# A hybrid RWKV-7 and sparse-attention layer: transposes of both heads in one bunch, value products in three bunches a pair, and fill work dealt out anew around the seam

## The chip, the cores and the metric

The kernel runs on one core of a Trainium2 chip. The metric is the device time of one execution in microseconds (us). The engines of the core are named as in the profile: PE (TensorE: matmuls and transposes into PSUM), PEld (its weight loads), DVE (VectorE), ACT (ScalarE), POOL (GpSimd, which here only touches SBUF) and SP (SyncE, which here issues most DMAs). Each engine works through its own instructions in the order in which they were issued.

## The reference

One decoder layer over 512 tokens of 1024 channels, in float32. Both mixers read one projection of the normalised stream:

```python
z = h @ w_in[l]
z_rwkv, z_nsa, z_gate = jnp.split(z, [RWKV_COLS, RWKV_COLS + NSA_COLS], axis=-1)
o_a = rwkv7_time_mix(z_rwkv, ...)
o_b = nsa_attention(z_nsa, ...)
g_a, g_b = jnp.split(jax.nn.sigmoid(z_gate), 2, axis=-1)
m = g_a * (o_a @ w_branch_rwkv[l]) + g_b * (o_b @ w_branch_nsa[l])
x = x + rms_norm(m @ w_out[l], norm_mix_post[l])
...
x = x + rms_norm((jax.nn.silu(u_gate) * u_val) @ ffn_down[l], norm_ffn_post[l])
```

`rwkv7_time_mix` is a linear recurrence over tokens with 16 heads of 64 channels. `nsa_attention` has 16 heads of 64, and its result is the gated sum of three causal attentions: over 31 compressed blocks, over selected blocks and over a sliding window. With 512 tokens the selection takes all blocks and the window reaches back to the start, so the last two are both plain causal attention, with keys and values of their own.

## The kernel before

Everything lies transposed, channels on the 128 partitions and the 512 tokens along the free axis. Large products are split: a float32 operand becomes a high and a low part in the type fp32r, and three matmuls (high by high, high by low, low by high) stand for one. Weights come by DMA as `raw`, ACT makes the high part, POOL the low part (line 160), both into rings of three buffers. A projection of 128 columns is 8 steps of 3 matmuls of 128x512 (lines 290 to 292).

The program is written as Python generators that are advanced in turn; a scheduler then sets the final order on each engine. `drive(fill, *threads)` advances the fill by one step and each thread at its own rate. "Fill" is work that PE can do at almost any time: the 16 sigmoid gates (`gates_`, outputs gt), the projections for q (`qproj`, one for each pair of heads), k and v, and the RWKV half of the branch product (`branch(0, ..)`, outputs ub00 to ub07, 24 matmuls each).

The stages in question:

- RWKV works on two groups of four head pairs (p = 0 to 3 and 4 to 7). Per pair, `prep` and `couple` build the operands: transposes into pb (line 140), then AR on DVE (line 549), then the products g from AR and KB (line 587). One gate is the fill beside the last pair of a group. Then `core(g)` inverts small triangles and runs the recurrence over eight chunks. Beside `core(0)` stand `NG0` = 10 gates and the inputs of pair 4; beside `core(1)` the last 4 gates, four v and two k projections and q0 to q3. `finish` normalises the output of a group and multiplies it by its gate (lines 817 to 849); for group 1 it runs beside the start of the attention.
- The seam: `score0` computes the scores of attention pair 0 with two steps of fill after each block; `vload` transposes the values (vtp).
- The attention runs over eight pairs of heads, p8 = 0 to 7. `score(p8 + 1)` and `values(p8)` are interleaved by a sorted list of fractions of a pair, with some steps of fill (table `FILL2`, with 16 for pairs 0 and 1). `score`: products s of q and k into the two banks of tag px, DVE adds the bias and takes the minimum (line 1056), ACT takes the exponent (line 1058), and `norm` scales each block by gate over sum, half of it on DVE and half on POOL (line 1034). `values`: the compressed part is transposed into pct and evicted as a split pair; then, in five groups `GRP` of one or two (branch, key block) parts, the blocks are transposed into pt (tag py, two banks), evicted into PT (six buffers, on ACT for the groups in `ONACT`, else on DVE), and multiplied by the values into acc, named o (line 1087). These products are float32 with 64 output columns a head; the two heads of a pair stand side by side in the array.
- Before pair `PX` = 2 all remaining fill is run (`run(fill)`), and `load_branch(0, ..)` starts to load RWKV's output and to split it into hh and hl (ACT line 1129, DVE line 1130), which the projections no longer need from there on. From pair 2 on the fill is `branch(0, ..)`.
- After pair 7 the rest of the fill runs, then `load_branch(1, ..)` splits the attention's output into sp, then `branch(1, ..)` (ub10 and on) follows.

In `values` each head's transposes are a step of their own, and the products of the group before stand between head 0's transposes and their eviction:

```python
if e == 0:
    products()
m.append(nw.tile([128, S], F32, tag="PT", name=f"PT{p8}{e}{k}", bufs=6))
```

Of the kernel before, what the change touches and what calls it, by code (L numbers as in the profile page):

```python
# [34 lines left out]
ID, IE, RD, RR, NG0, NQ1, PX, FN = (36, 36), (60, 60), (74, 74), (1.05, 0.85), 10, 4, 2, 1.6  # L35
NW, NU, PA = 13, 3, 0.25
GRP = (((0, 2), (1, 2)), ((0, 1), (0, 3)), ((0, 0),), ((1, 1), (1, 3)), ((1, 0),))
ONACT, FILL2 = (0, 2, 4, 5, 6, 8), (0, 0, 9, 10, 10, 10, 10, 15)
# [4 lines left out]
def hybrid_layer(ctx: ExitStack, tc: tile.TileContext, a, out, dbg=None, stop=None):  # L43
# [831 lines left out]
    for g in range(2):  # L875
        group_tiles(g)
        for i in range(GP):
            p = GP * g + i
            fill = [inputs(p + 1, os_[p + 1])] if i < GP - 1 else gates_(1)
# [60 lines left out]
    drive(itertools.chain(*gates_(16 - 2 - NG0, zp), *fr1, *[qproj(i) for i in range(NQ1)]), f0, *rt1)  # L940
# [72 lines left out]
    def score(p8, o):  # L1013
# [11 lines left out]
        def norm(e, qb):  # L1025
# [5 lines left out]
            for b in range(2):  # L1031
                for k in (qb + 1, qb):
                    i = b * 4 + k
                    (po if b else ve).tensor_scalar(o.pe[e, b, k], o.pe[e, b, k], st[e][:, 3, i:i + 1], None, op0=OP.mult)  # L1034
# [32 lines left out]

    def values(p8, o):
        g = p8 // 2
        acc = pz(f"o{p8}")  # L1070
        pt = py(f"pct{p8}")
# [5 lines left out]
        todo = []  # L1077

        def products(last=False):
            if not todo:  # L1080
                for x in range(2):
                    te.matmul(acc, vcp[:, g, x, :], pct, start=x == 0, stop=False)
                return
            m, parts = todo.pop()
            for b, j, c, n in parts:
                for e in range(2):
                    te.matmul(acc[e * 64:e * 64 + 64, j * 128:], vt[:, j, b * 256 + g * 64:b * 256 + g * 64 + 64],  # L1087
                              m[e][:, c:c + n], start=False, stop=last)

        for k, grp in enumerate(GRP):  # L1090
            m = []
            for e in range(2):
                pt = py(f"pt{p8}{e}{k}")
                parts, c = [], 0
                for b, j in grp:
# [6 lines left out]
                if e == 0:  # L1102
                    products()
# [5 lines left out]
                yield  # L1109
            todo.append((m, parts))  # L1110
        products(True)
        if p8 == 7:
            o.acc = acc
            return
        o8 = nw.tile([128, S], F32, tag="o8", name=f"o8{p8}", bufs=1)
        sc.activation(o8, acc, AF.Copy)
        sc.dma_start(obd[p8], o8)
# [14 lines left out]
    def branch(x, o8, sh, sl):  # L1132
# [3 lines left out]
        wh, wl = wslice(wh), wslice(wl)  # L1136
        p = pj(f"ub{x}{o8}")
# [22 lines left out]
    def score0():  # L1160
        for _ in score(0, os_[0]):
            for _ in range(2):
                next(fill, None)
            yield
# [347 lines left out]
```

## Time and profile before

| what | value |
|---|---|
| median of 3 runs | 1202.02 us (1200.98 to 1203.12) |
| profiled execution | 1201.8 us, its span 1200.0 us |
| RWKV up to the seam | 0 to about 502 us |
| score 0 and attention pairs 0 to 7 | about 502 to 739 us |
| branch products, output projection, MLP | about 739 to 1200 us |
| transposes pt of the attention, line 140 | 320, mean 274 ns |
| value products, line 1087 | 256 in the trace (each is two passes), mean 452 ns |

A row of the timeline or the chain begins with the start and the duration in us. The durations of single matmuls overlap, since PE pipelines them, so what one costs is read from the distance between starts, or from the chain of waits. "Waited for" means that PE stood idle until the engine named was done.

### The profile page before, as it was taken

The page shows a single profiled execution, that of the slowest core. Times are in us where ns is not written, and L with a number is a line of the kernel's source. Part 1 is how long each engine was busy: PE and PEld are TensorE (multiplying, and loading weights), DVE is VectorE, ACT ScalarE, POOL GpSimd, SP SyncE. Part 2 cuts the span into 40 slices and gives each one's busy share as a digit, 9 for nine tenths or more (in the row PEclk, how much of TensorE's full clock was granted, in tenths as well). Part 3 has the DMA queues.
Part 4 walks back from the last instruction along what each step waited for, and adds up shares of the span by engine and source line. Part 5 has one row for each costly group of instructions (what it writes and reads, how often), then busy time and mean ns, then how long its engine had stood idle before and what let it go on. Part 6 is the DMA issues. An engine that isn't in the chain of part 4 may idle for free.

```text
span 1200.0 us, 19851 instructions
## 1 busy us (share of the span) xinstructions
PE 1169.2 (97%) x7414; PEld 928.8 (77%) x7414; DVE 583.1 (49%) x1196; ACT 583.3 (49%) x1141; POOL 587.5 (49%) x529
## 2 busy tenths in 40 slices
PE   8999999999999999989999999999999999999997
PEld 6888878777877887767666776888888888888886
DVE  4225554537465452576777774754334333431103
ACT  5546553346665334466656664543444444443311
POOL 4336654445565444475465752621356655654440
PEclk8999999999899999999999999999999999999999
DMA  6522335411333553345332223751133333334421
GB/s 221 134 76 82 87 95 165 132 51 36 103 117 97 164 144 116 120 139 174 106 106 80 68 66 124 227 197 45 45 97 97 96 98 99 98 93 134 135 66 70
DMA packets 95651, 131.95 MB, mean 110 GB/s; under 512 B 34177, under 2 KB 37057, under 8 KB 95298
## 3 DMA queue, kind: packets, MB, share of 16 engines
q1 hardware_dynamic: 79634, 116.26, 32.0%
q10 hardware_dynamic: 15920, 14.42, 3.8%
q8 instruction: 58, 0.95, 0.3%
q14 instruction: 39, 0.32, 0.1%
HBM read 108.30 MB, written 19.14 MB: 106 GB/s over the span
## 4 chain that ended last, share of the span: by engine, by line
PE 84%; DVE 7%; issue 3%; ACT 3%; POOL 2%; DMA 1%; SPq 0%; DVEq 0%; POOLq 0%; ACTq 0%
PE pu L212 6%; PE pu L214 6%; PE pu L213 6%; PE dn L1245 3%; PE dn L1243 3%; PE dn L1244 3%; PE o L1087 3%; PE pt L140 3%; PE ub L1139 2%; PE ub L1140 2%; PE ub L1141 2%; PE v L290 2%; PE v L291 2%; PE v L292 2%; PE gt L292 2%
## 5 line engine op out<-in xcount | busy, mean ns | idle before, releaser
L1058 ACT ACTIVATE p<-p,stt 128x384 f32<-128x384 f32 (+3 forms) x128 | 70.8, 555 | 54.7 <-DVE stt L1056 54.3
L1034 POOL TENSOR_SCALAR p<-p,stt 128x512 f32<-128x512 f32 (+1 forms) x64 | 74.4, 1171 | 32.8 <-DVE stt L1029 25.2
L1383 DVE SCALAR_TENSOR_TENSOR u<-pu,cvec,u 128x511 f32<-128x511 f32 x44 | 33.0, 749 | 101.5 <-ACT u L1382 101.5
L1056 DVE CUSTOM_DVE_ANT_0 p<-s,rh 128x384 f32<-128x384 f32 (+3 forms) x128 | 58.5, 485 | 28.7 <-PE s L1051 17.4
L1087 PE MATMUL o<-PT,vt 128*64 128x384 f32 (+3 forms) x256 | 50.7, 452 | 1.1 <-DVE PT L1108 1.1
L140 PE MATMUL pt<-ident,p 128*128 128x128 f32 x320 | 49.1, 274 | 0.0
L1387 POOL TENSOR_TENSOR u<-u,u 128x512 f32<-128x512 f32 x22 | 28.4, 1290 | 38.3 <-DVE u L1384 37.3
L140 PEld LDWEIGHTS pt<-ident,p 128*128 128x128 f32 x320 | 39.8, 141 | 8.5 <-issue 0.4
L1389 DVE TENSOR_TENSOR al<-u,ah 128x512 fp32r<-128x512 f32 x22 | 23.9, 1085 | 45.5 <-ACT ah L1388 45.5
L1051 PE MATMUL s<-kst,qs 128*128 128x512 f32 (+1 forms) x128 | 36.9, 387 | 1.2 <-DVE stt L1056 0.8
L1382 ACT ACTIVATE u<-pu,cvec 128x512 f32<-128x512 f32 x44 | 33.6, 764 | 5.1 <-PE pu L1347 5.1
L1106 ACT ACTIVATE PT<-pt 128x512 f32<-128x512 f32 x48 | 28.0, 583 | 14.3 <-PE pt L140 12.2
L1034 DVE TENSOR_SCALAR p<-p,stt 128x512 f32<-128x512 f32 (+1 forms) x64 | 33.9, 563 | 0.9
L1384 DVE SCALAR_TENSOR_TENSOR u<-pu,cvec,u 128x510 f32<-128x510 f32 x44 | 33.0, 749 | 1.6
L1087 PEld LDWEIGHTS o<-PT,vt 128*64 128x64 f32 x256 | 16.9, 136 | 19.9 <-issue 14.5
L1108 DVE COPY PT<-pt 128x512 f32<-128x512 f32 x32 | 22.0, 687 | 18.4 <-PE pt L140 18.3
L1051 PEld LDWEIGHTS s<-kst,qs 128*128 128x128 f32 x128 | 22.7, 190 | 8.2 <-DVE stt L1056 2.8
L587 PEld LDWEIGHTS g<-AR,KB 64*128 64x128 f32 x256 | 19.8, 187 | 10.6 <-DVE GS L590 4.2
L1291 DVE TENSOR_TENSOR p2tm<-dn,gb 128x512 f32<-128x512 f32 x4 | 2.8, 692 | 51.2 <-ACT p2jl L1289 51.2
L587 PE MATMUL g<-AR,KB 64*128 64x128 f32 x256 | 23.0, 288 | 4.5 <-DVE AR L549 2.8
L1388 ACT ACTIVATE ah<-u 128x512 fp32r<-128x512 f32 x22 | 13.9, 633 | 22.3 <-POOL u L1387 22.3
L1058 ACT ACTIVATION_READ_ACCUMULATOR p<-p,stt 128x1 f32 x128 | 24.0, 188 | 0.0
(1757 smaller groups left out, 3957.7 us busy)
## 6 DMA issues: line engine op xcount, KB each, us to landing
gtd<-gt ACTq DMA_DIRECT2D x16, 256.0 KB, 2.4
qs<-qd SPq DMA_DIRECT2D x32, 128.0 KB, 3.0
g<-gtd SPq DMA_DIRECT2D x16, 256.0 KB, 3.5
xt<-in_x_dram SPq DMA_DIRECT2D x4, 512.0 KB, 5.1
bvd<-bv SPq DMA_DIRECT2D x8, 256.0 KB, 2.3
bvl<-bvd SPq DMA_DIRECT2D x8, 256.0 KB, 2.7
oad<-y SPq DMA_DIRECT2D x8, 256.0 KB, 2.6
kst<-kst ACTq DMA_DIRECT2D x16, 128.0 KB, 3.5
```

The lines of the kernel that those rows point to most:

```text
L140: return te.transpose(o, i, ident)
L212: te.matmul(p, wh(k), mh(k), start=first and k == 0, stop=False)
L213: te.matmul(p, wh(k), ml(k), start=False, stop=False)
L214: te.matmul(p, wl(k), mh(k), start=False, stop=last and k == n - 1)
L292: te.matmul(p, wl(k), hh[:, k, :], start=False, stop=k == KT - 1)
L587: te.matmul(gh[h][:, j * 128:(j + 1) * 128], KB[hs, c].rearrange("p s t -> p (s t)"), AR[hs, :, c * 64:(c + 1) * 64], start=True, stop=True)
L1034: (po if b else ve).tensor_scalar(o.pe[e, b, k], o.pe[e, b, k], st[e][:, 3, i:i + 1], None, op0=OP.mult)
L1051: te.matmul(s_[:, :n], qt, kt[:, x, b, :n], start=x == 0, stop=x == 1)
L1056: ve.tensor_tensor_reduce(sb, parts[b], rh[e][:, (3 - qb) * 128:], -1.0, BIG, OP.add, OP.min, st[e][:, 0, i:i + 1])
L1058: sc.activation(sb, sb, AF.Exp, scale=-1.0, bias=st[e][:, 0, i:i + 1], accum_out=st[e][:, 1, i:i + 1])
L1087: te.matmul(acc[e * 64:e * 64 + 64, j * 128:], vt[:, j, b * 256 + g * 64:b * 256 + g * 64 + 64], m[e][:, c:c + n], start=False, stop=last)
L1243: te.matmul(acc[half, t], sh[:, k, tsl], wh[kk], start=k == 0, stop=False)
```

## The change

Six edits go together:

- `values` now takes both heads of a group in one step (`turned(k)`): all transposes of the group, then both evictions. The products are called in three bunches: groups 0 and 1 behind the transposes of group 2 (with the two matmuls of the compressed part ahead of them), groups 2 and 3 behind those of group 4, and group 4's (`end`) behind the first transposes of the next pair, with the eviction and the store of acc. A pair has five steps instead of ten. pct moves from the banks of tag py to those of tag pz, which acc uses too. `ONACT` exchanges 5 for 7: of group 2 head 1 is evicted by DVE now, of group 3 head 1 by ACT.
- Gates: two instead of one beside the last pair of each RWKV group, 9 instead of 10 beside `core(0)`, 3 instead of 4 beside `core(1)`.
- `score0` takes 20 steps of fill instead of 16. In pair 0 (`p8` = 0) the scaling of head 0's second branch moves from POOL to DVE, four blocks.
- The fill is no longer run out ahead of pair 2: pairs 0 and 1 take 10 steps each instead of 16, the rest (9 steps) is spread over the first half of pair 2 and interleaved with `load_branch(0, ..)`, each load one place behind the projection step that reads the same slice of hh and hl.
- The first `branch(0, 0)` stops once behind its weights' loads and splits (at 0.3 of pair 2); its matmuls come from 0.5 on.
- The fill left after pair 7 is no longer run ahead of `load_branch(1, ..)` but between its steps.

```diff
-ID, IE, RD, RR, NG0, NQ1, PX, FN = (36, 36), (60, 60), (74, 74), (1.05, 0.85), 10, 4, 2, 1.6
+ID, IE, RD, RR, NG0, NQ1, PX, FN = (36, 36), (60, 60), (74, 74), (1.05, 0.85), 9, 4, 2, 1.6
-ONACT, FILL2 = (0, 2, 4, 5, 6, 8), (0, 0, 9, 10, 10, 10, 10, 15)
+ONACT, FILL2 = (0, 2, 4, 6, 7, 8), (10, 10, 6, 10, 10, 10, 10, 10)
...
-            fill = [inputs(p + 1, os_[p + 1])] if i < GP - 1 else gates_(1)
+            fill = [inputs(p + 1, os_[p + 1])] if i < GP - 1 else gates_(2)
...
-    drive(itertools.chain(*gates_(16 - 2 - NG0, zp), *fr1, *[qproj(i) for i in range(NQ1)]), f0, *rt1)
+    drive(itertools.chain(*gates_(16 - 4 - NG0, zp), *fr1, *[qproj(i) for i in range(NQ1)]), f0, *rt1)
...
-                    (po if b else ve).tensor_scalar(o.pe[e, b, k], o.pe[e, b, k], st[e][:, 3, i:i + 1], None, op0=OP.mult)
+                    (po if b and (p8 or e) else ve).tensor_scalar(o.pe[e, b, k], o.pe[e, b, k], st[e][:, 3, i:i + 1], None, op0=OP.mult)
...
+        pt = pz(f"pct{p8}")
         acc = pz(f"o{p8}")
-        pt = py(f"pct{p8}")
...
+        turned(0)
+        while behind_next:
+            behind_next.pop()()
+        yield
+        turned(1)
+        yield
+        turned(2)
+        for x in range(2):
+            te.matmul(acc, vcp[:, g, x, :], pct, start=x == 0, stop=False)
+        for k in range(2):
+            products(k)
+        yield
+        turned(3)
+        yield
+        turned(4)
+        for k in range(2, 4):
+            products(k)
+        yield
         if p8 == 7:
-            o.acc = acc
-            return
...
+            end()
+        else:
+            behind_next.append(end)
...
+        if x + o8 == 0:
+            yield
         p = pj(f"ub{x}{o8}")
...
-        for _ in score(0, os_[0]):
-            for _ in range(2):
+        for i, _ in enumerate(score(0, os_[0])):
+            for _ in range(3 - i % 2):
...
+            n = FILL2[p8]
+            order = [((i + 0.1) / 5, v) for i in range(5)] + [((i + 0.3) / 8, s) for i in range(8)]
+            if p8 == PX:
+                order += [(0.3, fill)]
+                order += [(0.05 * (i + 0.5), rest) for i in range(9)] + [(0.05 * (i + 1.5), load) for i in range(9)]
+                order += [(0.5 + 0.5 * (i + 0.5) / n, fill) for i in range(n)]
+            else:
+                order += [((i + 0.5) / n, fill) for i in range(n)]
...
         if p8 == PX - 1:
-            run(fill)
+            rest = fill
...
-    run(fill)
...
-        run(load_branch(1, obd, spb[0], spb[1], os_[7].acc))
+        load = load_branch(1, obd, spb[0], spb[1], os_[7].acc)
+        next(load)
+        for _ in fill:
+            next(load, None)
+        run(load)
```

Here `turned(k)` is the body of the old loop over groups with both heads in it, `products(k)` the old products of one group, and `end` the products of group 4 with the eviction and store of acc. Lines behind these edits shift: line 1087 of before is 1104 in the new kernel, 1139 to 1141 become 1161 to 1163, and 1082 becomes 1124.

How the issue order changes is shown at three places. First PE in pair 4, a steady pair, before: transposes of group 4 of head 0 (pt404, from the scaled blocks p80x), products of group 3 (o4 from PT403 of head 0 and PT413 of head 1), fill (ub03), transposes of head 1 (pt414).

```order
L140 MATMUL pt404_7194<-ident_89,p801_6861 128x128
L140 MATMUL pt404_7194<-ident_89,p811_6831 128x128
L140 MATMUL pt404_7194<-ident_89,p821_6740 128x128
L140 MATMUL pt404_7194<-ident_89,p831_6715 128x128
L1087 MATMUL o4_6955<-PT403_7155,vt_5263 64x384
L1087 MATMUL o4_6955<-PT413_7174,vt_5263 64x384
L1087 MATMUL o4_6955<-PT403_7155,vt_5263 64x128
L1087 MATMUL o4_6955<-PT413_7174,vt_5263 64x128
L1139 MATMUL ub03_7144<-hh_72,wb03h0_7132 128x512
L1140 MATMUL ub03_7144<-hl_73,wb03h0_7132 128x512
L1141 MATMUL ub03_7144<-hh_72,wb03l0_7133 128x512
L140 MATMUL pt414_7208<-ident_89,p901_6907 128x128
```

And PE at the same place behind the change, from the transposes of head 1 on (those of head 0 stand right ahead of them):

```order
L140 MATMUL pt414_7174<-ident_89,p901_6907 128x128
L140 MATMUL pt414_7174<-ident_89,p911_6869 128x128
L140 MATMUL pt414_7174<-ident_89,p921_6781 128x128
L140 MATMUL pt414_7174<-ident_89,p931_6760 128x128
L1104 MATMUL o4_6926<-PT402_7083,vt_5263 64x512
L1104 MATMUL o4_6926<-PT412_7090,vt_5263 64x512
L1104 MATMUL o4_6926<-PT403_7128,vt_5263 64x384
L1104 MATMUL o4_6926<-PT413_7135,vt_5263 64x384
L1104 MATMUL o4_6926<-PT403_7128,vt_5263 64x128
L1104 MATMUL o4_6926<-PT413_7135,vt_5263 64x128
L1161 MATMUL ub03_7202<-hh_72,wb03h0_7190 128x512
L1162 MATMUL ub03_7202<-hl_73,wb03h0_7190 128x512
```

The products of groups 2 and 3 now form one run, and the two heads' transposes another. Over the whole attention the order has 45 runs of products before and 30 behind the change, and 93 against 63 runs of transposes.

Second POOL during score 0, before: scalings of pair 0's blocks (line 1034), biases rh for pair 2, splits of `finish` (gl5, gl6 with their casts), and then the first split of the weights of q6.

```order
L822 CAST gh5_5513<-gl5_5514 32x128
L1034 TENSOR_SCALAR p131_5407<-p131_5407,stt1_5321 128x512
L1034 TENSOR_SCALAR p121_5445<-p121_5445,stt1_5321 128x384
L1021 TENSOR_SCALAR rh4_6037<-dist_5271 128x512
L1034 TENSOR_SCALAR p011_5478<-p011_5478,stt0_5318 128x256
L1034 TENSOR_SCALAR p001_5528<-p001_5528,stt0_5318 128x128
L1021 TENSOR_SCALAR rh5_6040<-dist_5271 128x512
L160 TENSOR_TENSOR gl6_5603<-g26r_5604,gh6_5602 128x256
L822 CAST gh6_5602<-gl6_5603 32x128
L1034 TENSOR_SCALAR p111_5543<-p111_5543,stt1_5321 128x256
L1034 TENSOR_SCALAR p101_5573<-p101_5573,stt1_5321 128x128
L160 TENSOR_TENSOR q6l0_5637<-q60r_5638,q6h0_5636 128x512
```

And POOL behind the change, from the end of the recurrence (SD16, YT1) to the first scaling:

```order
L777 TENSOR_TENSOR SD16_5177<-S16_5144,Dc1_3035 128x256
L751 TENSOR_TENSOR YT1_4804<-YT1_4804,gst1_4827 128x512
L160 TENSOR_TENSOR q6l0_5572<-q60r_5573,q6h0_5571 128x512
L751 TENSOR_TENSOR YT1_4804<-YT1_4804,gst1_4827 128x512
L1021 TENSOR_SCALAR rh0_5316<-dist_5271 128x512
L1021 TENSOR_SCALAR rh1_5319<-dist_5271 128x512
L1021 TENSOR_SCALAR rh2_5681<-dist_5271 128x512
L160 TENSOR_TENSOR q6l1_5578<-q61r_5579,q6h1_5577 128x512
L1021 TENSOR_SCALAR rh3_5684<-dist_5271 128x512
L817 TENSOR_TENSOR YT1_4804<-YT1_4804,gst1_4827 128x4x128 x4
L1034 TENSOR_SCALAR p131_5410<-p131_5410,stt1_5321 128x512
L1034 TENSOR_SCALAR p121_5451<-p121_5451,stt1_5321 128x384
```

Both of q6's splits have moved ahead of all scalings, and head 0's scalings (p031, p021, p011, p001) are gone from POOL. On PE, q5's 24 matmuls now all stand ahead of the first score; before, 18 of them stood between scores.

Third PE in the last pair of group 0, before: transposes into pb, fill (gt00), both transposes of V (pv30, pv31), then fill of the next gate (gt10).

```order
L140 MATMUL pb3_1713<-ident_89,nte3_1690 128x128 x4
L290 MATMUL gt00_1643<-hh_72,gt00h1_1650 128x512
L291 MATMUL gt00_1643<-hl_73,gt00h1_1650 128x512
L292 MATMUL gt00_1643<-hh_72,gt00l1_1651 128x512
L140 MATMUL pv30_1736<-ident_89,V3_1557 128x128 x4
L140 MATMUL pv31_1742<-ident_89,V3_1557 128x128 x4
L290 MATMUL gt10_1819<-hh_72,gt10h0_1820 128x512
```

And PE at that place behind the change:

```order
L140 MATMUL pb3_1713<-ident_89,nte3_1690 128x128 x4
L290 MATMUL gt00_1643<-hh_72,gt00h1_1650 128x512
L291 MATMUL gt00_1643<-hl_73,gt00h1_1650 128x512
L292 MATMUL gt00_1643<-hh_72,gt00l1_1651 128x512
L290 MATMUL gt10_1734<-hh_72,gt10h0_1735 128x512
L291 MATMUL gt10_1734<-hl_73,gt10h0_1735 128x512
L292 MATMUL gt10_1734<-hh_72,gt10l0_1736 128x512
```

The transposes of V come later, with fill between them; from pb to the products g (line 587) there are 24 fill matmuls instead of 19, and the same holds in the last pair of group 1.

More of the change, by code (lines that the diff above doesn't have):

```diff
@@ L1066, in score @@
         norm(*done.pop())
+    behind_next = []
     def values(p8, o):
         g = p8 // 2
+        pt = pz(f"pct{p8}")
         acc = pz(f"o{p8}")
-        pt = py(f"pct{p8}")
         for qb in range(4):
@@ L1076, in values, with turned @@
         ve.tensor_tensor(pct[64:128], pt[0:64], pct[0:64].bitcast(F32), op=OP.subtract)
[L1077 to L1082, printed above, removed]
-                return
[L1084 to L1091, printed above, removed]
+        PTs = []
+        def turned(k):
+            m, parts = [], []
             for e in range(2):
@@ L1094, in values @@
                 parts, c = [], 0
-                for b, j in grp:
+                for b, j in GRP[k]:
                     n = (4 - j) * 128
@@ L1101, in values @@
                     c += n
-                if e == 0:
-                    products()
                 m.append(nw.tile([128, S], F32, tag="PT", name=f"PT{p8}{e}{k}", bufs=6))
@@ L1108, in values, with products, end @@
                     ve.tensor_copy(m[e][:, :c], pt[:, :c])
-                yield
-            todo.append((m, parts))
-        products(True)
-        if p8 == 7:
-            o.acc = acc
[L1114 to L1117, printed above, removed]
+            PTs.append((m, parts))
+        def products(k):
+            m, parts = PTs[k]
+            for b, j, c, n in parts:
+                for e in range(2):
+                    te.matmul(acc[e * 64:e * 64 + 64, j * 128:], vt[:, j, b * 256 + g * 64:b * 256 + g * 64 + 64],
+                              m[e][:, c:c + n], start=False, stop=k == len(GRP) - 1)
+        def end():
+            products(4)
+            if p8 == 7:
+                o.acc = acc
+                return
+            o8 = nw.tile([128, S], F32, tag="o8", name=f"o8{p8}", bufs=1)
+            sc.activation(o8, acc, AF.Copy)
+            sc.dma_start(obd[p8], o8)
+        turned(0)
[16 more added lines that the diff above has]
+        yield
+        if p8 == 7:
+            end()
+        else:
+            behind_next.append(end)
     os_ = [P() for _ in range(8)]
@@ L1174, in steps @@
         def steps():
-            n = 16 if p8 < PX else FILL2[p8]
-            order = sorted([((i + 0.02) / 10, v) for i in range(10)] + [((i + 0.3) / 8, s) for i in range(8)]
-                           + [(0.25 + 0.75 * (i + 0.5) / n if p8 == PX else (i + 0.5) / n, fill) for i in range(n)]
-                           + [(0.02 + 0.06 * i, load) for i in range(9)], key=lambda x: x[0])
+            n = FILL2[p8]
[6 more added lines that the diff above has]
+                order += [((i + 0.5) / n, fill) for i in range(n)]
+            order.sort(key=lambda x: x[0])
             for _, x in order:
```

## The prediction

> **What bounds the kernel now.** First the page: TensorE (PE) is busy for 1169.2 of 1200.0 us, every other engine for about half, and the line of granted clocks shows 9 tenths or more in all but two slices (30 us each).
>
> ```profile
> span 1200.0 us, 19851 instructions
> PE 1169.2 (97%) x7414; PEld 928.8 (77%) x7414; DVE 583.1 (49%) x1196; ACT 583.3 (49%) x1141; POOL 587.5 (49%) x529
> PEclk8999999999899999999999999999999999999999
> ```
>
> So the time is PE's own work, its idle time (1200.0 - 1169.2 = 30.8 us), and what a lowered clock adds. A change can only win by giving PE less to do, or fewer waits. The waits of PE come next, over 480 to 760 us and then over 160 to 420 us (columns: who waits for whom, us in total, times, longest).
>
> ```profile
> PE ub L1141 <- POOL wb00l L160: 2.5, 1, 2.5
> PE q L292 <- POOL q6l L160: 1.8, 1, 1.8
> PE o L1082 <- DVE pct L1076: 1.2, 1, 1.2
> PE o L1087 <- DVE PT L1108: 1.1, 3, 0.6
> PE gt L140 <- DVE stt L1056: 1.0, 1, 1.0
> PE ub L1140 <- DVE sp L1130: 1.0, 2, 0.6
> PE s L1051 <- DVE stt L1056: 0.8, 1, 0.8
> PE pg L845 <- DVE stt L1056: 0.8, 1, 0.8
> ...
> PE g L587 <- DVE AR L549: 2.8, 2, 1.4
> ```
>
> Those are 13.0 us of the 30.8; most of the rest lies at the program's ends and behind the first recurrence. Third view, busy time by stretch (us of the stretch, then PE, PEld, DVE, ACT, POOL busy, granted clock, DMA share, GB/s): score 0, the two falls of the clock, pair 1, the start of pair 2, and two steady pairs.
>
> ```profile
> 502.50:521.00 18.50, 16.55 (x93) 13.23 (x92) 15.90 (x60) 15.54 (x44) 14.71 (x15) 1.00 0.50 171
> 525.00:528.00 3.00, 1.46 (x6) 1.24 (x7) 1.62 (x5) 1.30 (x3) 3.00 (x4) 1.00 0.53 178
> 528.00:531.50 3.50, 3.50 (x10) 2.02 (x8) 1.27 (x4) 2.04 (x5) 1.58 (x2) 0.51 0.37 122
> 557.80:588.00 30.20, 30.20 (x166) 21.50 (x164) 21.53 (x70) 18.24 (x50) 15.05 (x15) 1.00 0.47 149
> 588.00:600.00 12.00, 9.53 (x55) 6.50 (x53) 10.29 (x31) 9.31 (x23) 5.08 (x6) 1.00 0.34 109
> 603.00:606.60 3.60, 3.60 (x11) 2.58 (x10) 1.34 (x7) 1.25 (x4) 0.81 (x2) 0.53 0.74 233
> 644.00:694.00 50.00, 49.14 (x279) 34.66 (x278) 37.25 (x125) 30.62 (x87) 29.69 (x30) 1.00 0.20 62
> ```
>
> Two steady pairs: PE 49.14 of 50.00, DVE 37.25: PE bounds. In score 0 and at the start of pair 2 every engine is near full and PE waits; behind both the clock is halved for some 3.4 us, a loss of 1.7 us each time.
>
> **Fewer runs of value products.** The chain of waits prices a run in pair 7 (start us, us, what):
>
> ```profile
> 730.21 1.01 PE o L1087 x4
> 731.22 0.43 PE ub L1139
> 731.65 0.23 PE ub L1140
> ...
> 732.81 0.44 PE pt L140 x4
> 733.25 0.23 PE ub L1139
> ...
> 734.38 1.01 PE o L1087 x8
> 735.39 0.43 PE ub L1139
> ```
>
> Four transposes take 0.44, 0.11 for 128 columns, and the fill matmul behind them its usual 0.23: a bunch of transposes has no price of entry or exit, so bunching them saves nothing on PE. A run of products takes 1.01 whether it holds one part (x4, 512 columns a head) or two (x8, 384 and 128), and the matmul behind it 0.43 instead of 0.23. Two passes over 512 columns at the pace of the transposes are 2 x 4 x 0.11 = 0.87. A run thus carries 1.01 - 0.87 + 0.20 = **0.34 us** that does not grow with its contents. In the issue order there are 45 such runs before and 30 behind the change: pairs 1 and 3 to 7 have 3 (before 7, 5, 5, 5, 6, 5), pair 0 keeps 7 and pair 2 keeps 5. 15 x 0.34 = **-5.1 us**. The trace has no run of 1024 columns; the bounds are 15 x 0.20 = 3.0 (only the surcharge is saved) and 5.1. I take 5.1, because the boundary between two parts in the x8 run costs nothing.
>
> **Waits for PT and pct.** The evictions last (page, mean ns before the second bar):
>
> ```profile
> L1106 ACT ACTIVATE PT<-pt 128x512 f32<-128x512 f32 x48 | 28.0, 583 | 14.3 <-PE pt L140 12.2
> L1108 DVE COPY PT<-pt 128x512 f32<-128x512 f32 x32 | 22.0, 687 | 18.4 <-PE pt L140 18.3
> ```
>
> Products now come one bunch behind their transposes, and those with pct two bunches behind. The three waits for PT (1.1) go: **-1.1**. What takes their place is a wait of the evictions for PT buffers: the six are all held when bunch 2 is evicted, and bunch 3's evictions wait for the products of bunch 0. Those stand in PE's order right behind bunch 2, a fifth of a pair earlier, so I give new waits 0.2 us a pair, **+1.6** in all. The bounds are 0 and one eviction on DVE a pair, 8 x 0.69 = 5.5; PE has fill beside most bunches, which draws the value to the lower end. The deferred last products of a pair hold its acc and its store back by one bunch; the store is read only behind pair 7. The pct tile moves to the pz banks, whose two are reused a pair later: nothing. The ONACT swap sends one eviction each way: nothing.
>
> **Score 0 and pair 0.** Four scalings leave POOL for DVE, at the mean durations of the same line:
>
> ```profile
> L1034 POOL TENSOR_SCALAR p<-p,stt 128x512 f32<-128x512 f32 (+1 forms) x64 | 74.4, 1171 | 32.8 <-DVE stt L1029 25.2
> L1034 DVE TENSOR_SCALAR p<-p,stt 128x512 f32<-128x512 f32 (+1 forms) x64 | 33.9, 563 | 0.9
> 523.70 1.55 POOL L1034 TENSOR_SCALAR p<-p,stt 128x256 f32<-128x256 f32 x2
> 525.22 1.27 POOL L160 TENSOR_TENSOR q6l<-q60r,q6h 128x512 fp32r<-128x512 f32 x1
> 526.54 0.50 PE L292 MATMUL q<-hh,q6l 128*128 128x512 f32 x1 [1.80 <-POOL q6l L160]
> ```
>
> POOL is freed of 4 x 1.17 = 4.7 us, and in the new order q6's splits stand ahead of these scalings: the wait of 1.8 goes. DVE gets 4 x 0.56 = 2.3 more in a stage where it is busy for 15.9 of 18.5 and PE already waits for it (gt 1.0, pg 0.8). Also q5's fill, 18 of whose 24 matmuls stood between the first scores, is now all ahead of them; q6's matmuls replace it, but late in the stage. So the waits for DVE grow by 0 to 2.3; with 0.9, **-0.9** here. The half clock at 528 I leave in place.
>
> **Pair 2.** Before, its first part had no fill: PE waited 0.8 for scores, 1.2 for pct and 2.5 for wb00l. Now the 24 matmuls of the last key projection stand there, wb00's loads and splits are issued at 0.3 of the pair and its matmuls from 0.5. Of 4.5 us I leave 1.0: **-3.5**. The clock's fall at 603 follows the 2.5 us wait directly: **-1.7**. If conversions of RWKV's output, which write over hh and hl and so wait for those 24 matmuls, block ACT's queue, the 1.0 becomes 4.5.
>
> [...] The rows show a fall behind waits of 1.8 and 2.5 us, so I hold to them.
>
> **Ends of the recurrence's groups.** The last pair of each group gets a second gate.
>
> ```profile
> 172.34 0.39 PE L292 MATMUL gt<-hh,gt10l 128*128 128x512 f32 x1
> 172.57 0.39 PE L290 MATMUL gt<-hh,gt10h 128*128 128x512 f32 x1
> 174.37 1.16 PE L587 MATMUL g<-AR,KB 64*128 64x128 f32 x16 [1.41 <-DVE AR L549]
> ```
>
> In the new order 24 matmuls instead of 19 stand between the transposes into pb and these products: 5 x 0.23 = 1.15 of the 1.41, in both groups **-2.3**. The first recurrence gives up that gate: at worst 24 x 0.23 = 5.5 is missed where it ends, at best 2 us of its waits go, since the square root behind it no longer follows v5's second split in ACT's order. I take 0, nearest to those waits' present size.
>
> **The end.** 24 fill matmuls (5.5 us) now run behind the last products, beside the conversions for which PE waited twice (1.0): **-1.0**.
>
> **Sum.** -5.1 - 1.1 + 1.6 - 0.9 - 3.5 - 1.7 - 2.3 - 1.0 = -14.0. The profiled execution took 1201.8 (span 1200.0), 0.2 under the median of 1202.02, so **1187.8 us**.
>
> **Rivals.**
> 1. The seams exchange stalls: DVE's 2.3 and the bare scores bring PE's idle time between 500 and 620 and both falls of the clock back. Left are the runs, PT and the group ends, less DVE's 2.3: 1201.8 - 5.1 - 1.1 - 2.3 + 2.3 = 1195.6. For it: score 0 has little slack on any engine. Against it: POOL's splits come earlier for certain.
> 2. **Slower**: the early pairs turn out bound by DVE. The change takes 42 fill matmuls out of the attention (18 ahead of it, 24 behind it); if pairs do not get shorter by them, nor by the runs, they are pure addition: 42 x 0.23 = 9.7, less 2.3 and 1.0: 1208.2. It decides where DVE with its waits needs more than PE: in pair 1 PE's work falls to 30.2 - 18 x 0.23 - 4 x 0.34 = 24.7, against DVE's 21.5. 3.2 us of waits in DVE's chain would do it; the steady pairs run at 25 with 18.6 of DVE, which speaks against it.
> 3. The change does not do what it says for PE: the 0.34 belongs to each part rather than each run, and each wait gets a successor: 1201.8 - 2.3 = 1199.5 to 1202.
> [...]
>
> **How the numbers follow.** Forecast 0.62, rival 1 0.18, rival 2 0.09, rival 3 0.08, rival 4 0.03. About 0.2% (2.4 us) is what a measurement of this kernel tells from no change. Faster takes the forecast, rival 1 and a little of 3 and 4: 0.83; same 0.08; slower 0.09. The range reaches from 1181 (the 0.9 and 1.6 gone to their good ends, the first recurrence 2 better, the other clock fall gone as well) to 1198, over rival 1.
>
> **What would show it.** In the new profile: product runs of 1024 columns at 1.9 us with one 0.43 behind each; no wait for PT or wb00l; g waiting for AR 0.3 a time; the granted clock of 600 to 610 at 1.00; a steady pair 0.7 us shorter than now. Wrong it would be with PE idle for over 9 us in the first 120 us of the attention, or with steady pairs no shorter.

## The result and the profile after

| | median us (lowest to highest, runs) | before on the same chip, us | ratio to before (95%) |
|---|---|---|---|
| before | 1202.07 (1200.98 to 1203.12, 4) | | |
| changed | 1186.83 (1184.63 to 1188.66, 4) | 1202.07 | 0.9873 (0.9853 to 0.9892) |
| changed, second series | 1185.04 (1183.18 to 1187.00, 4) | 1202.66 | 0.9852 (0.9837 to 0.9866) |
| forecast | 1187.8 (1181.0 to 1198.0) | | |

The change makes the kernel 15.2 us faster in the first series and 17.6 in the second; the forecast was 14.2 (its sum of -14.0, taken from the profiled execution of before). The profiled execution of the changed kernel took 1184.63 us, 2.2 under the median of its series. Its page (span, busy time, and the granted clock in 40 slices):

```profile
span 1182.8 us, 19859 instructions
PE 1156.4 (98%) x7414; PEld 925.3 (78%) x7414; DVE 578.7 (49%) x1200; ACT 582.6 (49%) x1141; POOL 580.2 (49%) x525
PEclk8999999999999999999999999999999999999999
```

The 17.2 us between the spans split into two parts here. PE's idle time went from 30.8 to 1182.8 - 1156.4 = 26.4 us, 4.4 less. PE's busy time went from 1169.2 to 1156.4, 12.8 less, and part of that is the clock. Between 100 and 1100 us the trace of before records four windows of 3.4 us at half clock (two from 299.4 us, one at 528.1, one at 603.2); this trace of the changed kernel records none. Such a window loses up to 1.7 us of PE's work, 6.8 in all (an estimate from the length and the granted clock, 3.4 us at 0.50; from 303.6 us matmuls of 128x512 follow each other every 0.43 us, and every 0.23 behind 306.7, at the full clock); 12.8 - 6.8 = 6.0 us is then less work. The forecast's terms, sorted in the same way, were 7.2 for waits, 1.7 for the clock and 5.1 for work.

PE's waits in the changed kernel, over 480 to 760 us (who waits for whom: us in total, times, longest):

```profile
PE s L1051 <- DVE stt L1056: 3.7, 9, 0.8
PE pg L845 <- ACT y L839: 1.3, 1, 1.3
...
PE ub L1163 <- POOL wb14l L160: 0.6, 1, 0.6
...
PE ub L1163 <- POOL wb13l L160: 0.2, 1, 0.2
...
PE ub L1163 <- POOL wb15l L160: 0.2, 1, 0.2
```

and over 160 to 420 us:

```profile
PE xs L792 <- DVE UV L786: 1.1, 1, 1.1
...
PE g L587 <- DVE AR L549: 0.5, 2, 0.2
```

The waits for wb00l, q6l, pct and PT are gone. The one for AR at the group ends fell from 2.8 to 0.5. Grown is one kind: scores (L1051) that wait for DVE to have read the score before them, nine times instead of once (0.8). The chain of waits near the end of the changed kernel's attention shows the merged run:

```profile
703.87 0.87 PE pt L140 x8
704.74 0.46 PE o L1124 x2
705.21 1.88 PE o L1104 x16
707.08 0.43 PE ub L1161
```

Four parts in one run (1024 columns a head) take 1.88 us, with one surcharge of 0.20 behind them: less than two runs of 1.01 with two surcharges by 0.34, as forecast.

### The profile page after: what moved, and what is told of

Its sections match the earlier page's. It is cut to its first block, busy times and chain, and to the rows that moved or that the text cites. A ratio compares the mean times of both kernels' runs of the same rounds, so it can differ in the third digit from the quotient of the medians.

```text
span 1182.8 us, 19859 instructions
## 1 busy us (share of the span) xinstructions
PE 1156.4 (98%) x7414; PEld 925.3 (78%) x7414; DVE 578.7 (49%) x1200; ACT 582.6 (49%) x1141; POOL 580.2 (49%) x525
## 4 chain that ended last, share of the span: by engine, by line
PE 82%; DVE 6%; issue 3%; ACT 3%; POOL 2%; DMA 2%; SPq 0%; ACTq 0%; DVEq 0%; POOLq 0%
PE pu L212 6%; PE pu L213 6%; PE pu L214 6%; PE dn L1275 3%; PE dn L1273 3%; PE dn L1274 3%; PE o L1104 3%; PE pt L140 3%; PE v L290 2%; PE gt L291 2%; PE gt L290 2%; PE ub L1161 2%; PE gt L292 2%; PE ub L1163 2%; PE v L292 2%
## 5 line engine op out<-in xcount | busy, mean ns | idle before, releaser
L1034 POOL TENSOR_SCALAR p<-p,stt 128x512 f32<-128x512 f32 (+3 forms) x60 | 68.5, 1152 | 35.1 <-DVE stt L1029 25.8
L140 PE MATMUL pt<-ident,p 128*128 128x128 f32 x320 | 44.6, 273 | 0.2 <-DVE p L1034 0.2
L1104 PE MATMUL o<-PT,vt 128*64 128x384 f32 (+3 forms) x256 | 43.4, 444 | 0.0
L1051 PE MATMUL s<-kst,qs 128*128 128x512 f32 (+1 forms) x128 | 38.2, 390 | 3.7 <-DVE stt L1056 3.7
L1034 DVE TENSOR_SCALAR p<-p,stt 128x512 f32<-128x512 f32 (+1 forms) x68 | 35.1, 559 | 0.6
L1104 PEld LDWEIGHTS o<-PT,vt 128*64 128x64 f32 x256 | 17.2, 136 | 18.8 <-issue 16.5
L1051 PEld LDWEIGHTS s<-kst,qs 128*128 128x128 f32 x128 | 21.4, 188 | 12.7 <-DVE stt L1056 7.9
```

The lines of the kernel that those rows point to most:

```text
L140: return te.transpose(o, i, ident)
L1034: (po if b and (p8 or e) else ve).tensor_scalar(o.pe[e, b, k], o.pe[e, b, k], st[e][:, 3, i:i + 1], None, op0=OP.mult)
L1051: te.matmul(s_[:, :n], qt, kt[:, x, b, :n], start=x == 0, stop=x == 1)
```

## The experiments

There are three parts to tell apart: the value products, the gates, and the seams (score 0, pair 2, the end). Each part alone, and the changed kernel with five runs a pair, were measured on one chip beside a before of 1202.83 us.

### The value products alone

```diff
 # the kernel before, with values(), ONACT and the five steps of v of the changed one
-            order = sorted([((i + 0.02) / 10, v) for i in range(10)] + ...
+            order = sorted([((i + 0.1) / 5, v) for i in range(5)] + ...
```

> The kernel before, with the new value products alone (transposes of both heads in one bunch, products in three bunches, the last of them behind the next pair's first transposes); both seams, the fill and the gates stay as they were. The issue order has 30 runs of products instead of 45. Theory of the prediction: -5.1 for 15 runs at 0.34 us, -1.1 for the waits for PT and +1.6 for new ones, so 1197.4 us. Reading of the changed kernel's trace: PE's work between the first score and the last product, without its waits, its lowered clocks and the 42 fill matmuls that left, fell by 6.2 us; by that 0.41 a run and no new wait for PT, so 1194.7. Rival: the price belongs to each part and not to each run, 1200 to 1202. The falls of the clock near 300, 528 and 603 us should all still be there, since their waits are.

Measured: 1193.02 us (1190.45 to 1193.68), ratio 0.9914 (0.9900 to 0.9928): 9.8 us faster, twice what the prediction gave this part. The stretch from the first scores to the first matmul of ub10 shows where that lies. A row gives the stretch and its length, the busy time of PE, PEld, DVE, ACT and POOL with the number of instructions, the granted clock, and the DMA's share and GB/s. First the kernel before and this one, then the same stretches for the value products alone (PE and PEld only):

```profile
502.60:739.20 236.60, 226.89 (x1235) 160.46 (x1233) 165.30 (x524) 143.66 (x387) 139.07 (x137) 0.99 0.33 104
502.60:730.10 227.50, 218.37 (x1235) 160.37 (x1233) 161.45 (x524) 142.76 (x387) 138.59 (x137) 0.98 0.35 108
...
502.60:739.20 236.60, 50.64 (x256) 16.87 (x256) 0.99 0.33 104
502.60:730.10 227.50, 42.33 (x256) 16.25 (x256) 0.98 0.35 108
```

The stretch is 9.1 us shorter. PE's idle time in it fell by only 0.6 (9.7 to 9.1) and its busy time by 8.5; the view of the products alone shows 8.3 less. Fifteen runs at 0.37 (next experiment) are 5.5 of the 8.5. Most of the rest is a cost that the prediction did not price. In the kernel before, three runs stop in the middle to wait for PT, here the one with the longest wait:

```profile
652.87 0.86 PE L1087 MATMUL o<-PT,vt 128*64 128x384 f32 x2
654.32 1.08 PE L1087 MATMUL o<-PT,vt 128*64 128x384 f32 x6 [0.59 <-DVE PT L1108]
```

A run of this content takes 1.01 us in one piece. Here one head's part takes 0.86 by itself, and behind the wait the rest takes 1.01 all the same, because the two heads no longer run side by side. So each of the three runs (at 627.9, 652.9 and 678.2 us) costs 0.86 us of busy time beside its wait, 2.6 in all, and the new kernel has no such run: 5.5 + 2.6 = 8.1 of the 8.5.

The waits of this kernel between 480 and 760 us, the two longest:

```profile
PE s L1051 <- DVE stt L1056: 2.6, 6, 0.7
PE ub L1161 <- POOL wb00l L160: 1.7, 1, 1.7
```

With pair 2's fill exactly as before, the waits of that pair (0.8, 1.2 and 2.5) have shrunk to the one of 1.7. So a large part of what the prediction put down to pair 2's new order comes with the value products already: they no longer hold up PE in front of pct. Other waits, those of scores for DVE above all, have taken their place.

### What a run costs: five runs a pair again, and the heads apart

```diff
 # the changed kernel; each bunch's products in a run of their own
         turned(1)
+        (the two products with pct)
+        products(0)
         yield
-        turned(2)
-        ...
+        for k in range(1, 4):
+            turned(k + 1)
+            products(k)
+            yield
```

> The changed kernel, with the products of each part bunch in a run of their own right behind the next bunch of transposes: five runs a pair, 45 instead of 30 in the issue order, all else alike. Theory of the prediction: 15 x 0.34 = 5.1 us more, 1191.9 us. By 0.41 a run 1193.0. Rival: the run has no price of its own and the shorter pairs come from elsewhere (order, waits): 1186.8 us.

Measured: 1190.79 us (1189.94 to 1193.35), ratio 0.9904 (0.9890 to 0.9918): 4.0 and 5.8 us more than the two series of the changed kernel. In the second kernel the transposes are taken apart and the products keep their three bunches. In its issue order scores cut four of these, so that it has 34 runs instead of 30:

```diff
 # the changed kernel; ten steps a pair instead of five
-        def turned(k):
-            for e in range(2):
+        def turned(k, e):
...
+            turned(k, 0)
+            yield
+            turned(k, 1)
```

> The changed kernel with the transposes of the two heads of a group issued in steps of their own, ten a pair: 92 bunches of transposes in the issue order instead of 63, the products still in three bunches a pair (34 runs instead of 30, the four more in pairs 0, 1, 3 and 5). Theory of the prediction, that bunching transposes saves nothing on PE: only the four runs, 4 x 0.36 = 1.4 us more than the 1185 to 1187 us of the changed kernel. Rival: a steady pair with five product runs but bunched transposes did 0.38 us less work than the pair before the change, and if that is the transposes' it comes back too: 8 x 0.38 = 3.0 and 1.4, 4.4 us more.

Measured: 1189.21 us (1187.40 to 1192.43), ratio 0.9899 (0.9883 to 0.9914): 2.4 to 4.2 us more.

Pairs 4 and 5 are the place to read both, since their content is the same in all four kernels. Busy time of that stretch, from the first score issued in pair 4 to that of pair 6, first the kernel before:

```profile
643.82:694.14 50.32, 49.46 (x282) 34.96 (x282) 37.57 (x125) 30.79 (x88) 30.01 (x30) 1.00 0.20 63
```

the changed kernel with five runs a pair:

```profile
634.43:684.00 49.57, 48.70 (x282) 34.71 (x282) 37.30 (x124) 30.20 (x87) 29.79 (x30) 1.00 0.21 65
```

the changed kernel with the heads apart:

```profile
631.44:679.61 48.17, 47.78 (x283) 34.93 (x282) 38.17 (x125) 30.05 (x88) 30.11 (x30) 1.00 0.24 74
```

and the changed kernel:

```profile
629.01:676.98 47.97, 47.23 (x282) 34.97 (x282) 35.80 (x124) 30.14 (x87) 30.01 (x30) 1.00 0.21 67
```

The count of matmuls is the same (282, one more recorded in one trace). From five runs to three, four runs less in two pairs, PE's busy time falls by 48.70 - 47.23 = 1.47: **0.37 us a run**, where the prediction had 0.34. With the heads apart it is 47.78 - 47.23 = 0.55 more, but not by the transposes: in this stretch scores cut the last run of pair 3, and the chain shows what that costs.

```profile
633.27 1.00 PE o L1105 x2
634.27 0.66 PE s L1051 x2
634.93 1.00 PE o L1105 x2
...
658.73 1.01 PE o L1105 x4
```

Each head alone takes 1.00 us, as long as both together in the last row (the same run of pair 4, in one piece). The cut thus costs 1.0, more than the whole 0.55. From the first run of pair 4 to that of pair 5 neither kernel has a cut; first the changed kernel, then the one with the heads apart:

```profile
638.24:662.35 24.11, 23.56 (x143) 17.55 (x144) 17.90 (x62) 15.09 (x45) 15.99 (x17) 1.00 0.23 77
643.46:667.28 23.82, 23.43 (x143) 17.39 (x144) 20.33 (x63) 14.76 (x44) 16.43 (x17) 1.00 0.26 78
```

Taking the heads apart costs no busy time there (23.43 against 23.56), so the prediction's sentence that bunching transposes saves nothing stands. The rival's 0.38 a pair is not the transposes'. Over the whole attention (500 to 750 us) this kernel's products take 46.18 us and those of the changed kernel 43.39; these 2.8 us, which come with the four runs more, cover most of the 2.4 to 4.2.

With five runs the two pairs are 49.46 - 48.70 = 0.76 shorter than before the change, with as many runs. Two of the three interrupted runs of before lie there, 1.7 us; so about 1.0 came back in PE's other matmuls, and no run here says why.

### The products with pct by themselves

```diff
 # the changed kernel; the two products with pct behind turned(1)
         turned(1)
+        for x in range(2):
+            te.matmul(acc, vcp[:, g, x, :], pct, start=x == 0, stop=False)
         yield
         turned(2)
-        for x in range(2):
-            te.matmul(acc, vcp[:, g, x, :], pct, start=x == 0, stop=False)
```

> The changed kernel with the two products with pct issued by themselves behind the second bunch of transposes, instead of right ahead of the first run of value products; all else alike. Theory of the prediction, which gave their place no price: no difference from the changed kernel. Rival: they, too, pay for an entry and an exit where they stand alone, about 0.3 us a pair, 2.4 us more.

Measured: 1187.46 us (1186.34 to 1189.43), ratio 0.9883 (0.9868 to 0.9897). That is 0.6 over the first series of the changed kernel and 2.4 over the second; its interval overlaps that of the first and lies just beside that of the second, so time does not decide. Its pairs 4 and 5 say no to the rival, with 47.26 busy against 47.23:

```profile
631.73:679.28 47.55, 47.26 (x283) 35.19 (x282) 36.18 (x124) 30.30 (x87) 29.86 (x30) 1.00 0.23 67
```

Elsewhere it has a cost of another kind: at 598.6 us, in pair 2, scores cut a run between the heads, and over the whole attention its products take 44.47 us against 43.39.

### The gates alone, and undone

```diff
-NG0 = 10          fill = ... gates_(1)      gates_(16 - 2 - NG0, zp)
+NG0 = 9           fill = ... gates_(2)      gates_(16 - 4 - NG0, zp)
```

> The kernel before, with the three edits of the gates alone (two gates at each group's last pair, nine behind the first group). Theory of the prediction: -2.3 at the two group ends, 1199.7 us, the falls of the clock near 300 us stay. Rival, from the changed kernel's trace: the new place of the gates also reorders the end of the first recurrence, and it is this that takes both half-clock windows near 300 us (2 x 1.7) away: with 3.5 at the group ends 1195.1 us, and the granted clock is 1.00 there in the profile.

> The changed kernel with the three edits of the gates undone. Theory of the prediction: 2.3 us more, 1189.1 us. By the gates alone on the kernel before (-5.5) 1192.3 us. In between: the group ends and the first recurrence lose 5.5, but 18 matmuls of q5 stand between the first scores again and take 2 us of waits out of score 0: 1190.3 us.

Measured: 1197.34 us (1194.61 to 1198.90), ratio 0.9954 (0.9941 to 0.9967), so 5.5 us for the gates alone; undone in the changed kernel 1190.34 us (1188.78 to 1190.88), ratio 0.9894 (0.9879 to 0.9908), 5.3 us slower than the changed kernel beside it. The prediction had 2.3. The longest wait over 160 to 420 us with the gates undone:

```profile
PE g L587 <- DVE AR L549: 2.8, 2, 1.4
```

The 2.8 for AR is back to the digit (0.5 in the changed kernel), so 2.3 was right as the price of the group ends. The rest fits the clock behind the first recurrence, as these three rows show for 299.40 to 306.20 us: the kernel before,

```profile
299.40:306.20 6.80, 6.32 (x31) 4.96 (x32) 3.52 (x6) 2.23 (x4) 1.43 (x2) 0.50 0.22 41
```

the gates alone,

```profile
299.40:306.20 6.80, 6.80 (x34) 5.61 (x33) 1.44 (x2) 3.10 (x6) 2.89 (x5) 1.00 0.58 195
```

and the changed kernel with the gates undone:

```profile
299.40:306.20 6.80, 6.22 (x30) 4.86 (x31) 3.52 (x6) 2.20 (x5) 1.42 (x2) 0.50 0.21 36
```

All four profiled kernels with the old gates have the half clock there for 6.8 us (a granted clock of 0.50 in their two rows above and of 0.52 over the same stretch with the value products alone), a loss of up to 3.4; of the ten profiles with the new gates one has it (at 295.5 us, in the kernel with pair 2 as before). The runs without a profile agree: with the gates undone, the mean granted clock is 0.991 to 0.994 in all four executions, and 0.996 to 0.999 in the four of the changed kernel beside it. 2.3 and 3.4 make 5.7, against 5.3 and 5.5 measured. The rival was right and the prediction's "I take 0" for the first recurrence was not.

### The seams: alone, and all of them left out

```diff
 # seams alone: the kernel before with
+            for _ in range(3 - i % 2):          # score 0's fill
+FILL2 = (10, 10, 6, 10, 10, 10, 10, 10)         # and pair 2, the end, L1034
 # left out: the kernel before with the new value products and the new gates only
```

> The kernel before, with the edits of score 0, pair 2 and the end alone (old value products, old gates). Theory of the prediction: -0.9 at score 0, -3.5 at pair 2, -1.7 for the clock at 603 us, -1.0 at the end: 1194.9 us. Rival, from the changed kernel's trace: of its 17.2 us 7.3 belong to the value products, 3.5 to the group ends, 3.4 to the clock near 300 us, which leaves 3.0 for the seams: 1199 us. The profile shows no wait of 2.5 us for wb00l in either case; the falls near 300 us stay.

> The kernel before with the new value products and the three edits of the gates, and none of the edits of score 0, pair 2 and the end. Theory of the prediction: the seams are worth 7.1 us (0.9 at score 0, 3.5 and 1.7 at pair 2, 1.0 at the end), so it is 7 us behind the changed kernel, 1192 to 1193. Rival: the value products alone gave 9.8 and the gates alone 5.5, which with nothing lost between them is 1187.5, and the seams bring the last 1 to 2 us.

Measured: alone 1199.99 us (1198.03 to 1201.11), ratio 0.9981 (0.9969 to 0.9993), 2.8 us faster; left out 1193.52 us (1192.42 to 1196.19), ratio 0.9934 (0.9920 to 0.9949), 6.7 and 8.5 us behind the changed kernel. Alone, the rival was close (1199), and the prediction's 1194.9 was not; as the last part, the prediction was close (1192 to 1193), and the rival's 1187.5 was not. So neither theory holds by itself: the same edits are worth 3 us or 7 to 8, depending on what stands beside them. Put alone, their gain is taken by the old value products, as the waits over 480 to 760 us of the first kernel show:

```profile
PE o L1082 <- DVE pct L1076: 3.0, 4, 1.3
PE o L1087 <- DVE PT L1108: 2.2, 5, 0.6
```

These were 1.2 and 1.1 before: with less fill between them the old products run into their operands more often, and the products themselves take 53.26 us instead of 50.72 (500 to 750 us). Left out, on the other hand, value products and gates (9.8 and 5.5 by themselves) do not add up at all: 1193.5 is no better than the value products alone, 1193.0. The waits over 480 to 760 us of that kernel:

```profile
PE s L1051 <- DVE stt L1056: 4.0, 8, 0.8
PE q L292 <- POOL q6l L160: 2.4, 1, 2.4
PE pt L140 <- POOL p L1034: 2.2, 2, 1.3
PE ub L1161 <- POOL wb00l L160: 1.7, 1, 1.7
```

The new gates put the rest of q5 ahead of the first score. With the old fill two steps a block remain for score 0, and what is missing shows as waits: scalings on POOL, then q6l for 2.4 us because POOL does the scalings first:

```profile
527.00 1.51 POOL L1034 TENSOR_SCALAR p<-p,stt 128x256 f32<-128x256 f32 x2
528.48 1.27 POOL L160 TENSOR_TENSOR q6l<-q61r,q6h 128x512 fp32r<-128x512 f32 x1
```

The wait for q6l is followed by half a clock (third and fourth row; the first two are score 0, with a half-clock window of its own at 505.6 us, and pair 0):

```profile
502.70:525.40 22.70, 18.31 (x95) 13.49 (x94) 17.84 (x63) 17.31 (x48) 14.58 (x16) 0.92 0.38 124
525.40:560.00 34.60, 32.19 (x166) 22.62 (x165) 24.78 (x74) 20.62 (x54) 23.87 (x26) 0.95 0.49 157
526.10:529.50 3.40, 1.29 (x8) 0.69 (x5) 3.19 (x9) 1.34 (x3) 3.23 (x5) 1.00 0.88 302
529.50:532.90 3.40, 3.10 (x9) 2.57 (x10) 0.99 (x2) 0.96 (x3) 0.25 (x1) 0.50 0.37 133
```

In the changed kernel the same two stages by busy time, and behind them q6l's split in POOL's timeline:

```profile
501.50:524.70 23.20, 19.50 (x104) 14.52 (x104) 20.05 (x69) 18.59 (x50) 12.72 (x15) 1.00 0.47 156
524.70:553.50 28.80, 27.25 (x147) 18.36 (x145) 22.23 (x70) 18.32 (x50) 19.94 (x21) 1.00 0.44 138
```

```profile
501.71 1.27 POOL L160 TENSOR_TENSOR q6l<-q61r,q6h 128x512 fp32r<-128x512 f32 x1
```

Score 0 takes nine matmuls more in 0.5 us more, since PE had the time. Pair 0 has 19 fewer and is 5.8 us shorter: 19 x 0.23 = 4.4 by the matmuls that it no longer has, and up to 1.7 by the clock. q6's second split lies 27 us earlier. But work that moves to a later pair is not saved. What the seams bring is read from the whole stretch up to ub10, in which both kernels have the same matmuls; first the kernel without the seams' edits, then the changed one:

```profile
502.30:730.90 228.60, 217.41 (x1217) 156.53 (x1216) 162.26 (x524) 143.04 (x387) 136.54 (x135) 0.99 0.34 106
501.10:721.80 220.70, 213.40 (x1218) 155.62 (x1218) 168.60 (x534) 144.55 (x391) 130.76 (x130) 1.00 0.36 112
```

The changed kernel is 7.9 us shorter there: PE's idle time is 3.9 less (11.2 to 7.3) and its busy time 4.0 less, of which the two half-clock windows make up to 3.4. So the gain is waits and clock, and hardly any work. Rival 2's mechanism is seen here in part: in score 0 fill costs little, and taking it out hardly shortens that stage.

### The seams undone one by one

On one chip with the second series of the changed kernel (1185.04 us), and the end in a series of its own (before: 1202.29 us):

```diff
 # pair 2 as before
+            n = 16 if p8 < PX else FILL2[p8]          FILL2 = (16, 16, 9, 10, ...)
+            run(fill)                                 # instead of rest = fill
 # L1034 as before
+                    (po if b else ve).tensor_scalar(...)
 # the end as before
+    run(fill)
+        run(load_branch(1, obd, spb[0], spb[1], os_[7].acc))
```

> The changed kernel with pair 2 as before: 16 steps of fill in pairs 0 and 1, the rest of the fill run out ahead of pair 2, the branch's loads and matmuls in the old places, no early split of wb00. Theory of the prediction: 3.5 for waits and 1.7 for the clock come back, 1192.0 us. Rival: the new value products alone have taken most of pair 2's waits away (in their run the three waits of 0.8, 1.2 and 2.5 had become one of 1.7), so that 1.0 for waits and about half a fall of the clock are left: 1188.7 us.

> The changed kernel with the four scalings of pair 0 back on POOL. Theory of the prediction: the wait for q6l of 1.8 comes back and 0.9 of DVE's waits go: 1187.7 us. Rival: DVE's 2.3 us are what the first scores wait for (0.76, 0.79 and 1.00 us in the changed kernel's profile), and the new order of the fill has taken q6l's wait away by itself: 1185.3 us.

> The changed kernel with its end as before: the fill that is left runs out ahead of the second branch's loads, which then follow in one go. Theory of the prediction: the waits of 1.0 us for the conversions come back, 1 us more than the changed kernel. Rival: the changed kernel's end waits as long as that for weights (L1163 for wb13l to wb15l, 1.0 us in its first profile), so no difference.

| undone | median us (lowest to highest) | ratio to before (95%) |
|---|---|---|
| pair 2 | 1185.74 (1184.75 to 1187.96) | 0.9855 (0.9838 to 0.9871) |
| L1034 on DVE | 1185.04 (1184.86 to 1187.91) | 0.9857 (0.9842 to 0.9872) |
| the end | 1185.50 (1184.79 to 1187.77) | 0.9871 (0.9854 to 0.9888) |

None of the three can be told from the changed kernel. Pair 2, forecast at 5.2 us, is worth 0.7 by the medians; the intervals leave room for some 2 to 3 us, so even the rival's 3.7 was too much. Without its new order the waits that come back in pair 2 are

```profile
PE ub L1161 <- POOL wb01l L160: 1.2, 1, 1.2
...
PE ub L1161 <- POOL wb00l L160: 0.4, 1, 0.4
```

1.6 us instead of the 4.5 before the change, and the changed kernel pays elsewhere: its pg waits 1.3 for y, in a pair 0 that has less fill. L1034: with the scalings back on POOL no wait for q6l returns, so it was the place of the split in POOL's order that removed it, not the time that POOL was given. The end: its kernel keeps the last 10 of `FILL2`, so the fill that the prediction priced still runs behind pair 7, and only its interleaving with the loads is undone; the waits for the conversions do not come back.

Of the seams, then, the three and two steps of fill a block in score 0 are left as what brings the 7 to 8 us. That is by exclusion, and the exclusion is weak: parts that stand in for each other would also show nothing when they are undone one by one. A kernel with that edit alone taken out was not tried, so which of the seams' edits brings the gain stays open.

### The changed kernel again

> The changed kernel itself, beside the next three on one chip. By the runs so far 1186.8 us. In its first profile the clock never fell between 20 and 1180 us. [...] Rival: the falls hang on the order of the work alone, and this profile again shows none.

Measured: 1185.04 us (first table). Its profile has one fall of the clock that the first did not have, here with the 3.40 us ahead of it:

```profile
502.60:506.00 3.40, 1.86 (x9) 1.22 (x9) 2.27 (x8) 2.99 (x6) 3.28 (x4) 1.00 0.87 312
506.00:509.40 3.40, 3.38 (x11) 2.53 (x11) 2.93 (x10) 2.38 (x7) 2.83 (x3) 0.50 0.02 5
```

The rival was wrong: the same program shows a fall in one execution and not in the next, so the order of the work alone does not decide.

## Why the prediction came out right

The sum was close (-14.0; measured -15.2 and -17.6), and in part by luck: its terms missed in both directions. The value products alone brought 9.8 where the prediction had 4.6, the gates 5.5 where it had 2.3, and the seams alone 2.8 where it had 7.1. Together these make 18.1, and the three parts took some of it from each other.

- **Fewer runs, -5.1: right in mechanism and size.** 0.37 us a run against 0.34; 15 x 0.37 = 5.5, and taking the merge back cost 4.0 to 5.8.
- **Transposes in one bunch, nothing: right.** Bunches of four (0.44) and of eight (0.87) show the same 0.11 a transpose, and with the heads apart the stretch without a cut run did not get longer.
- **Waits for PT, -1.1 + 1.6: mis-sized.** It priced the three waits by PE's idle time (1.1). Each also interrupted a run and cost 0.86 of busy time, 2.6 more. As for the new waits, no eviction makes PE wait. The scores wait for DVE, 3.7 us in nine waits, of which the view by lines puts 2.0 between 502 and 526 us. That leaves 1.7 for the pairs: the size was right, the cause not.
- **Score 0, -0.9: too small, as far as the runs tell.** It priced waits and left the half clock behind q6l's wait in place. Without the seams' edits, idle time and clock together cost some 7 us more from the first scores to ub10; score 0's share of it is not isolated.
- **Pair 2, -3.5 and -1.7: the waits went, but not through this edit.** The new value products took most of them, and with the edit undone the time is the same within 2 to 3 us. The prediction read each part against the kernel before and so counted a wait for one part that another part removes.
- **Ends of the groups, -2.3: right** (2.8 to 0.5 in the waits). **First recurrence, 0: wrong**: up to 3.4 us of half clock hung on the gate that was moved.
- **The end, -1.0: not seen.** The waits for the conversions went; waits for wb13l to wb15l (1.0 in all) stand there now.
- **Rival 1** (seams exchange stalls) describes the waits of the kernel with the seams alone: the one for wb00l went, and those for pct and PT grew from 2.3 to 5.2. It had both falls of the clock back, and that kernel has no fall between 310 and 1100 us (its profile's mean granted clock is 0.993, against 0.990 before). **Rival 2** holds in part in score 0 of the kernel without the seams' edits. **Rival 3** falls with 0.37 a run. For the 0.03 that the forecast gives to a rival 4 no run shows a ground: the granted clock through pairs 4 and 5 is 1.00.

The two signs of being wrong did not come: PE idled 6.4 us in the first 120 us of the attention (over 9 was the mark), and a steady pair is 1.2 us shorter (0.7 was forecast).

Not settled: 15 runs at 0.37 and three interruptions at 0.86 make 8.1 us, and PE's busy time lost 6.0 beside the clock. Pairs 4 and 5 show such a return, too (1.0 us in matmuls other than the products). What makes these longer the runs do not say.

## What to carry to other kernels

A pause of one engine often has several owners: price a change that has several parts in the state that the other parts leave behind, not against the kernel before, and undo the parts one by one as well as doing them alone (the seams: 2.8 us alone, 7 to 8 as the last part; pair 2: 5.2 forecast, 0.7 when undone). Price a wait not by its idle time alone: one that stops a run of products between two heads cost 0.86 us of work besides, and a pair of scores issued between them 1.0. A split that feeds a matmul should be issued ahead of the other work on its engine: its place in POOL's order took q6l's wait away here, with or without the scalings on POOL.

## What the hardware showed

**Where the clock fell.** By the record of granted clocks, a fall lasted 3.4 or 6.8 us at 0.50: in the kernel before 6.8 from 299.4 us, and 3.4 each from 528.1 and 603.2. The starts lie 228.7 and 75.1 us apart there, and 221.9 with the value products alone (299.1 and 521.0); 228.7 / 67, 75.1 / 22 and 221.9 / 65 are all 3.41. What ties them to this step the runs do not show. The stretch right ahead of a fall was not idle: in the 3.40 us ahead of those at 506.0 us (the changed kernel again) and 529.5 us (without the seams' edits) PE was busy for 1.86 and 1.29 us. Nor does that share decide by itself; here, with the value products alone, 1.76 of 3.40 was followed by the full clock:

```profile
599.50:602.90 3.40, 1.76 (x10) 1.37 (x11) 3.40 (x12) 0.97 (x3) 2.51 (x3) 1.00 0.15 49
602.90:606.30 3.40, 3.40 (x17) 2.06 (x19) 1.67 (x10) 3.10 (x10) 2.18 (x2) 1.00 0.88 257
```

What else decides stays open. Nor does a lower clock always show in the time: of the four executions in the second series of the changed kernel, the one with the lowest mean granted clock, 0.996, was the fastest with 1183.18 us, and the two with 0.999 took 1184.58 and 1185.51; the first profile of the changed kernel has 0.996, too, without a half-clock window from 100 to 1100 us. For a forecast it means that a wait of 1 to 2.5 us carries a chance of up to 1.7 us more, not a sure loss, and that one profile shows only one draw of it: the fourteen profiles of this study have between none (the first of the changed kernel) and four (the kernel before) such half windows from 100 to 1100 us.

**Two heads side by side cost one.** A product for one head with 64 output columns over 512 tokens took 1.00 us alone, and the products for two heads issued together 1.01. In the trace of before the stop for PT, and in that of the heads apart two scores, came between the two, and PE paid for both heads one after the other (0.86 and 1.01 us, and twice 1.00). The trace counts that as busy time, so no list of waits shows it.
